# Two late modulation rows: from TensorE products to sums on VectorE

## The chip, the cores and the metric

One core of a Trainium2 chip runs the whole layer. The metric is the device time of one execution in microseconds (us), as the median of several runs; the profile is that of one further execution. The engines are called as the profile calls them: PE is TensorE's matmuls and PEld its weight loads, DVE is VectorE, ACT is ScalarE, POOL is GpSimd, and SP is the engine whose queue issues most of the DMA loads. Each engine works through its instructions in a fixed order and waits where an operand is missing.

## The reference, cut to what matters

The layer computes six modulation rows from one vector, uses two of them in the first norm, one as the gate of the first residual, two in the second norm and one as the gate of the second residual:

```python
mod = jax.nn.silu(c) @ w_ada[i] + b_ada[i]                  # (1, 1024) @ (1024, 6144)
sh1, sc1, g1, sh2, sc2, g2 = jnp.split(mod[:, None, :], N_MOD, axis=-1)
h = modulate(rmsnorm(x, norm1_g[i]), sh1, sc1)
...                                                          # projection, attention, long convolution
x = x + g1 * gated_merge(...)
h2 = modulate(rmsnorm(x, norm2_g[i]), sh2, sc2)
x = x + g2 * swiglu(h2, ffn_w1[i], ffn_w3[i], ffn_w2[i])
```

All is in float32. The parts are numbered 0 to 5 in the order of the split, so parts 2 and 5 are the gates g1 and g2, and parts 3 and 4 are the shift and scale of the second norm. The weight of one part is 1024 by 1024, 4 MB.

## The kernel before, in words

The kernel goes through these stages: the first norm and the input projection (40 chunks of 128 output columns; each chunk is two halves of 512 tokens, and a half is 24 products of 128x128 by 128x512, `gemm`, line 195); beside the projection a second stream of work, `side`; then attention, the merge of the branches, the second norm and the feed-forward network.

The second stream first makes the filters of the long convolution (`filters`) together with the late modulation rows (`ada_rows`, the function that is changed), and then runs the four convolutions (`conv`). `filters` goes four times through the same steps: products of the filter network (`filt_ps`, line 363) times a decay table that is loaded in tiles (`dec`, line 359; the product is `fv`, line 370), folds on DVE (lines 378 to 430, the last of them writes `a`), Fourier products on PE (`dft_ps`, lines 442 to 444), a copy by ACT, and a store of the spectrum by SP (`spec<-ks`, line 390). The convolutions use the same folds and Fourier products and begin with the load of `u` (line 454). Their tiles take the memory that the pool of the filters and the modulation rows has had.

The projection's weights come through one raw buffer (`wr`, loaded by SP, line 181), which ACT casts to a high part (`wh`, line 175) and DVE splits into a low part (`wl`, line 176). For the convolution's chunks DVE also adds the taps of a short convolution (line 600), and PE turns the result to tokens (`tm_ps`, line 569).

In `ada_rows` the rows are made in two pairs, (3, 4) and then (2, 5). For a pair, a row tile `arow` takes the biases from memory (line 882). For each part and each of the eight blocks k of 128 input channels, SP loads a weight tile `wal` of 128 by 1024 (512 KB, line 887), in three buffers. Four products (line 889) multiply it by the column of silu(c) of that block: the stationary operand is 128x32, with silu(c) in its first column, and each of the four works on 256 columns in a strip of 32 columns of the array, so part n of the pair ends up in rows 0, 32, 64 and 96 and columns 256n to 256n + 255 of one PSUM tile `ar_ps`, which is held until the pair is done. DVE adds it to `arow` (line 893), POOL writes the rows to memory (line 896). The first pair is then also turned into columns for the second norm. The gate rows are read back much later: g1 before the merge's output (line 1002), g2 in the feed-forward's second half (line 1367).

The order of the work is set in two steps. Generators yield estimated costs, and `_merged` takes the next step from the stream that is furthest behind its share; filters (97) and rows (39) are merged so, and the whole side stream (496) with the projection (39 chunks). The order that results is the order of the program. When the program is built, a planner with its own estimate of durations then gives each engine a fixed order: among what is ready and has its buffers it takes what comes first in the program, so that projections fill PE's time where a fold is not ready. Weight loads and taps are raised in priority; a few instructions are kept in program order.

Of the kernel before, what the change touches and what calls it, by code (L numbers as in the profile page):

```python
# [10 lines left out]
F32 = mybir.dt.float32  # L11
F32R = mybir.dt.float32r
AF = mybir.ActivationFunctionType
ALU = mybir.AluOpType
# [4 lines left out]
P = 128  # L19
D = 1024  # L20
# [138 lines left out]
class Block:  # L159
# [712 lines left out]
    def ada_rows(self, pool, psf):  # L872


        nc, a = self.nc, self.a
        for pair in ((3, 4), (2, 5)):
            r = pool.tile([P, 512], F32, tag="arow", name="arow", bufs=1)
            nc.gpsimd.memset(r, 0.0)
            for n, part in enumerate(pair):
                for j in range(4):  # L880
                    at = part * D + 256 * j
                    nc.gpsimd.dma_start(r[32 * j:32 * j + 1, 256 * n:256 * n + 256], a["b_ada"][0:1, at:at + 256])
            ps = psf.tile([P, 512], F32, tag="f", name="ar_ps")
            for n, part in enumerate(pair):
                for k in range(8):
                    w = pool.tile([P, D], F32, tag="wal", name="wal", bufs=3)
                    nc.sync.dma_start(w, a["w_ada"][k, :, part * D:(part + 1) * D])
                    for j in range(4):
                        nc.tensor.matmul(ps[32 * j:32 * j + 32, 256 * n:256 * n + 256], self.cs[:, 2 * k:2 * k + 32],
                                         w[:, 256 * j:256 * j + 256], start=(k == 0), stop=(k == 7),  # L890
                                         tile_position=(0, 32 * j))
                    yield 1.2
            nc.vector.tensor_add(r, ps, r)
            for n, part in enumerate(pair):
                for j in range(4):
                    nc.gpsimd.dma_start(self.modd[part][0:1, 256 * j:256 * j + 256],
                                        r[32 * j:32 * j + 1, 256 * n:256 * n + 256])
            if pair[0] == 3:
                pt = psf.tile([P, 512], F32, tag="f", name="ada_t")
                for j in range(4):  # L900
                    nc.tensor.transpose(pt[:, j * P:(j + 1) * P], r[:, j * P:(j + 1) * P], self.ident)
                v = pt.rearrange("p (n h g q) -> p n q g h", n=2, h=2, g=4)[:, :, 0]
                cols = lambda t: t.rearrange("p (g h) -> p g h", h=2)
                nc.vector.tensor_copy(cols(self.mod2[:, 1, :]), v[:, 0])
                nc.vector.scalar_tensor_tensor(cols(self.mod2[:, 0, :]), v[:, 1], 1.0, cols(self.ng[:, 1, :]),
                                               op0=ALU.add, op1=ALU.mult)
# [207 lines left out]
    def sums(self, wa, psf, xs, raw, h2):  # L1114

        nc = self.nc
        for k in range(4):
            b = []
            for kk in (k, k + 4):
                pt = psf.tile([P, 512], F32, tag="f", name="hT_ps")  # L1120
                for j in range(4):
                    mm = nc.tensor.transpose(pt[:, j * P:(j + 1) * P], xs[j][:, kk * P:(kk + 1) * P], self.ident)
                    if j == 0:
                        self.tc.keep_in_program_order(mm)
                h = wa.tile([P, 512], F32, tag="t", name="htmp")
                nc.scalar.activation(h, pt, AF.Identity, bias=self.mod2[:, 1, kk:kk + 1],
                                     scale=self.mod2[:, 0, kk:kk + 1])
                b.append(h)
            put = lambda n, src: self.split(h2[n][0][:, k, :], h2[n][1][:, k, :], src)
            b12, b22 = b  # L1130
            b11, b21 = raw[:, k, :], raw[:, k + 4, :]
            nc.vector.tensor_sub(b11, b12, b11)
            put(5, b11)
            nc.vector.tensor_sub(b12, b22, b12)
            put(7, b12)
            nc.vector.tensor_sub(b11, b22, b11)
            put(6, b11)
            put(3, b22)
            nc.vector.tensor_sub(b21, b21, b11)
            put(4, b21)  # L1140
            yield
# [312 lines left out]
```

## Time and profile before

| | before |
|---|---|
| median of 3 runs | 1719.76 us (1718.63 to 1722.28) |
| profiled execution | 1721.66 us, span 1719.9 us |
| PE busy | 1669.8 us, 97% of the span |
| DVE busy | 1187.3 us, 69% |
| ACT busy | 662.2 us, 39% |
| POOL busy | 152.7 us, 9% |
| mean granted TensorE clock | 0.995 |

The span goes from the first to the last instruction. Busy shares are means over stages that differ, so a stage has to be read by itself. The rows of a group give line, engine, operation, what is written and read, shape and count, then busy us and mean ns of one, then the idle time before them and what ended it. The filters and the modulation rows take the time from about 76 to 330 us of the span, the convolutions the time from there to about 660.

### The profile page before, as it was taken

How to read it: one execution, taken by the hardware profiler on the slowest of the kernel's cores; microseconds unless marked ns; L12 is line 12 of the kernel's file. 1: busy time of each engine (PE TensorE's matmuls, PEld its weight loads, DVE VectorE, ACT ScalarE, POOL GpSimd, SP SyncE). 2: the span in 40 equal slices, each digit the busy share in tenths (PEclk: the TensorE clock that was granted, in tenths of full speed). 3: DMA queues.
4: the chain of work that ended last, by engine and by line, in shares of the span. 5: the costliest groups of instructions: out<-in, count | busy, mean ns of one | idle time of the engine just before them, and what ended most of it. 6: DMA issues, size and time to landing. Idle time of an engine off the chain costs nothing.

```text
span 1719.9 us, 22909 instructions
## 1 busy us (share of the span) xinstructions
PE 1669.8 (97%) x8348; PEld 1311.0 (76%) x8348; DVE 1187.3 (69%) x2006; ACT 662.2 (39%) x1141; POOL 152.7 (9%) x273
## 2 busy tenths in 40 slices
PE   6999999999999999999999999999999999999997
PEld 2766766777777777888787788788888888878886
DVE  3665266699995966565865867867866566479566
ACT  4711222312221224455654325733333333355455
POOL 0100210101010004020200001010101001100000
PEclk9999999999999999999999999999999999999999
DMA  9375556645554456344657524333432323395344
GB/s 357 108 252 198 170 196 207 216 159 180 172 180 157 159 178 193 125 144 129 202 171 241 165 68 165 129 122 129 153 105 94 108 92 105 111 381 176 99 121 153
DMA packets 109910, 282.51 MB, mean 164 GB/s; under 512 B 15327, under 2 KB 24163, under 8 KB 107493
## 3 DMA queue, kind: packets, MB, share of 16 engines
q1 hardware_dynamic: 89864, 219.99, 38.2%
q0 software_dynamic: 19280, 60.60, 10.5%
q8 instruction: 66, 1.08, 0.3%
q10 hardware_dynamic: 653, 0.44, 0.1%
q14 instruction: 47, 0.39, 0.1%
HBM read 213.60 MB, written 67.39 MB: 163 GB/s over the span
## 4 chain that ended last, share of the span: by engine, by line
PE 44%; issue 26%; DVE 5%; DMA 5%; POOL 3%; ACT 1%; SPq 0%; POOLq 0%; ACTq 0%; DVEq 0%
PE in_ps L195 11%; PE out_ps L1091 5%; PE dx_ps L1322 5%; PE x_ps L1153 4%; PE dz_ps L1322 3%; PE dft_ps L442 2%; PE hy_ps L195 2%; PE pt_ps L800 2%; PE pt_ps L786 2%; PE na_ps L195 1%; POOL g L1266 1%; DMA ar<-g 1%; PE dft_ps L443 1%; PE dy_ps L1322 1%; PE dft_ps L444 1%
## 5 line engine op out<-in xcount | busy, mean ns | idle before, releaser
L195 PE MATMUL in_ps<-hTh,wl 128*128 128x512 f32 x640 | 259.3, 406 | 2.1 <-ACT proj L614 1.7
L195 PE MATMUL in_ps<-hTh,wh 128*128 128x512 f32 x640 | 253.2, 396 | 0.0
L195 PE MATMUL in_ps<-hTl,wh 128*128 128x512 f32 x640 | 252.6, 395 | 0.3 <-DVE hTl L176 0.2
L195 PEld LDWEIGHTS in_ps<-hTh,wl 128*128 128x128 f32 x640 | 120.7, 189 | 33.6 <-issue 5.1
L195 PEld LDWEIGHTS in_ps<-hTh,wh 128*128 128x128 f32 x640 | 120.8, 189 | 28.0 <-issue 1.6
L195 PEld LDWEIGHTS in_ps<-hTl,wh 128*128 128x128 f32 x640 | 120.9, 189 | 26.7 <-DVE hTl L176 1.9
L176 DVE TENSOR_TENSOR wl<-wr,wh 128x1024 fp32r<-128x1024 f32 (+1 forms) x56 | 59.8, 1068 | 95.7 <-ACT wh L175 95.6
L175 ACT CAST wh<-wr 128x1024 fp32r<-128x1024 f32 (+1 forms) x56 | 51.9, 926 | 135.6 <-PE in_ps L195 109.1
L176 DVE TENSOR_TENSOR ol<-ws,oh 128x512 fp32r<-128x512 f32 x88 | 60.4, 688 | 48.7 <-ACT oh L175 48.5
L176 DVE TENSOR_TENSOR ol<-ar,oh 128x512 fp32r<-128x512 f32 x77 | 52.8, 688 | 47.0 <-ACT oh L175 47.0
L175 ACT CAST oh<-ar 128x512 fp32r<-128x512 f32 x77 | 47.9, 622 | 83.6 <-PE dx_ps L1322 33.1
L175 ACT CAST oh<-ws 128x512 fp32r<-128x512 f32 x88 | 54.7, 622 | 57.5 <-PE x_ps L1153 27.4
L775 ACT ACTIVATE pe<-pe,mx 128x640 f32<-128x640 f32 x64 | 52.6, 823 | 49.3 <-DVE mx L774 49.3
L1322 PE MATMUL dx_ps<-ol,oh 128*128 128x512 f32 x176 | 68.7, 390 | 1.7 <-DVE ol L176 1.7
L442 PE MATMUL dft_ps<-a,matf 128*128 128x512 f32 x128 | 66.2, 598 | 4.0 <-DVE a L430 3.1
L1322 PE MATMUL dx_ps<-oh,ol 128*128 128x512 f32 x176 | 67.3, 390 | 2.0 <-DVE ol L176 2.0
L774 DVE CUSTOM_DVE_ANT_0 pe<-s_ps,bias 128x640 f32<-128x640 f32 x64 | 50.1, 820 | 27.7 <-PE s_ps L769 27.7
L1322 PE MATMUL dx_ps<-oh 128*128 128x512 f32 x176 | 68.5, 389 | 0.0
L175 ACT CAST oh<-wr 128x512 fp32r<-128x512 f32 x70 | 43.3, 622 | 51.5 <-PE x_ps L1153 16.0
L176 DVE TENSOR_TENSOR ol<-wr,oh 128x512 fp32r<-128x512 f32 x70 | 48.0, 688 | 21.2 <-ACT oh L175 21.0
L370 DVE TENSOR_TENSOR fv<-filt_ps,dec 128x512 f32<-128x512 f32 x32 | 21.5, 688 | 51.7 <-DMA dec<-in_decay 32.1
L1093 DVE TENSOR_TENSOR x<-x,out_ps 128x512 f32<-128x512 f32 x64 | 42.7, 684 | 19.1 <-PE out_ps L1091 18.9
(391 smaller groups left out, 4191.4 us busy)
## 6 DMA issues: line engine op xcount, KB each, us to landing
wr<-in_w SPq DMA_DIRECT2D x52, 512.0 KB, 3.6
wr<-in_w_in SPq DMA_DIRECT2D x40, 512.0 KB, 4.5
ar<-g SPq DMA_DIRECT2D x77, 256.0 KB, 2.8
wal<-in_w_ada SPq DMA_DIRECT2D x32, 512.0 KB, 6.6
matf<-in_dft_f SPq DMA_DIRECT2D x32, 384.0 KB, 4.4
bias<-in_rpb SPq DMA_DIRECT2D x64, 192.0 KB, 3.7
g<-t POOLq DMA_DIRECT2D x47, 256.0 KB, 3.0
w<-in_w SPq DMA_DIRECT2D x44, 256.0 KB, 5.4
```

The source lines that it names most:

```text
L175: self.nc.scalar.copy(hi, src)
L176: self.nc.vector.tensor_sub(lo, src, hi.bitcast(F32))
L195: mm = nc.tensor.matmul(ps, ww[:, k * P:(k + 1) * P], xx[:, k, pos:pos + width], start=(i == 0), stop=(i == n - 1))
L442: nc.tensor.matmul(ps, m[:, 0], v.rearrange("p a b -> p (a b)"), start=True, stop=False)
L774: nc.vector.tensor_tensor_reduce(pe, ps[:, 256:896], bt, -1.0, 3e38, ALU.add, ALU.min, mx[:, 0:1])
L775: nc.scalar.activation(pe, pe, AF.Exp, bias=mx[:, 0:1], scale=-1.0, accum_out=mx[:, 1:2])
L786: pin(nc.tensor.transpose(pt[:, at:at + P], pe[:, c * P:(c + 1) * P], self.ident))
L800: pin(nc.tensor.matmul(pt[ch, 1280:1408], vv[:, ch], pts[:, hh, c * P:(c + 1) * P], start=(c == 0), stop=(c == 4), tile_position=(0, 64 * ...
L1091: nc.tensor.matmul(ps, gg[x][:, tk], ww[y][:, sl], start=(i == 0), stop=(i == n - 1))
L1093: nc.vector.tensor_add(x1[:, sl], x1[:, sl], ps)
L1153: mm = nc.tensor.matmul(ps, w[u][:, k * P:(k + 1) * P], x[v][:, k, :], start=(start and k == 0 and i == 0), stop=(stop and k == 3 and i == 2),
L1322: nc.tensor.matmul(ps[j], x[u][:, j * P:(j + 1) * P], w[v], start=(start and i == 0 and c == 0), stop=(stop and i == N - 1 and k == len(re ...
```

## The change

The first pair, parts 3 and 4, is computed as before, now in the inner generator `products`. The second pair, the gates, goes through the new generator `sums`. It splits each part in two halves of 512 columns. For a half it loads eight tiles of 128 by 512 (256 KB) and sums them on DVE: the first is multiplied by its block's column of silu(c), and each further one is multiplied and added to the accumulator `aacc` (128x512). The accumulator still holds one sum for each of 128 partitions, so two products with a stationary block of ones (128x32) add over the partitions, 256 columns each, in two strips of 32; DVE adds the 64 rows that hold them to `arow`. The tag `wal` has two buffers for both pairs, where it had three; a half-width tile takes a full-width buffer. The yielded costs of the pair sum to the same 19.2. Biases, stores and everything behind stay.

```diff
 def ada_rows(self, pool, psf):
+        ones = pool.tile([P, 32], F32, name="ones", tag="ones", bufs=1)
+        nc.gpsimd.memset(ones, 1.0)
+        def products(r, pair):
+            ...
+                    w = pool.tile([P, D], F32, tag="wal", name="wal", bufs=2)
+            ...
+        def sums(r, pair):
+            for n, part in enumerate(pair):
+                for h in range(2):
+                    acc = pool.tile([P, 512], F32, tag="aacc", name="aacc", bufs=2)
+                    for k in range(8):
+                        w = pool.tile([P, D], F32, tag="wal", name="wal", bufs=2)[:, 0:512]
+                        at = part * D + 512 * h
+                        nc.sync.dma_start(w, a["w_ada"][k, :, at:at + 512])
+                        c = self.cs[:, 2 * k:2 * k + 1]
+                        if k:
+                            nc.vector.scalar_tensor_tensor(acc, w, c, acc, op0=ALU.mult, op1=ALU.add)
+                        else:
+                            nc.vector.tensor_scalar(acc, w, c, None, op0=ALU.mult)
+                        yield 0.6
+                    ps = psf.tile([P, 512], F32, tag="f", name="ar_ps")
+                    for j in range(2):
+                        g = 64 * h + 32 * j
+                        nc.tensor.matmul(ps[g:g + 32, 0:256], ones, acc[:, 256 * j:256 * j + 256], start=True,
+                                         stop=True, tile_position=(0, g))
+                    rs = r[64 * h:64 * h + 64, 256 * n:256 * n + 256]
+                    nc.vector.tensor_add(rs, ps[64 * h:64 * h + 64, 0:256], rs)
 ...
-            ps = psf.tile([P, 512], F32, tag="f", name="ar_ps")
-            for n, part in enumerate(pair):
-                for k in range(8):
-                    w = pool.tile([P, D], F32, tag="wal", name="wal", bufs=3)
-                    ...
-            nc.vector.tensor_add(r, ps, r)
+            yield from (products if pair[0] == 3 else sums)(r, pair)
```

More of the change, by code (lines that the diff above doesn't have):

```diff
@@ L875, in ada_rows @@
         nc, a = self.nc, self.a
+        ones = pool.tile([P, 32], F32, name="ones", tag="ones", bufs=1)
[5 more added lines that the diff above has]
+                    w = pool.tile([P, D], F32, tag="wal", name="wal", bufs=2)
+                    nc.sync.dma_start(w, a["w_ada"][k, :, part * D:(part + 1) * D])
+                    for j in range(4):
+                        nc.tensor.matmul(ps[32 * j:32 * j + 32, 256 * n:256 * n + 256], self.cs[:, 2 * k:2 * k + 32],
+                                         w[:, 256 * j:256 * j + 256], start=(k == 0), stop=(k == 7),
+                                         tile_position=(0, 32 * j))
+                    yield 1.2
+            nc.vector.tensor_add(r, ps, r)
+        def sums(r, pair):
+            for n, part in enumerate(pair):
+                for h in range(2):
+                    acc = pool.tile([P, 512], F32, tag="aacc", name="aacc", bufs=2)
+                    for k in range(8):
+                        w = pool.tile([P, D], F32, tag="wal", name="wal", bufs=2)[:, 0:512]
[7 more added lines that the diff above has]
+                        yield 0.6
+                    ps = psf.tile([P, 512], F32, tag="f", name="ar_ps")
+                    for j in range(2):
[4 more added lines that the diff above has]
+                    nc.vector.tensor_add(rs, ps[64 * h:64 * h + 64, 0:256], rs)
         for pair in ((3, 4), (2, 5)):
@@ L882, in ada_rows @@
                     nc.gpsimd.dma_start(r[32 * j:32 * j + 1, 256 * n:256 * n + 256], a["b_ada"][0:1, at:at + 256])
-            ps = psf.tile([P, 512], F32, tag="f", name="ar_ps")
-            for n, part in enumerate(pair):
-                for k in range(8):
-                    w = pool.tile([P, D], F32, tag="wal", name="wal", bufs=3)
[L887 to L893, printed above, removed]
+            yield from (products if pair[0] == 3 else sums)(r, pair)
             for n, part in enumerate(pair):
```

## The prediction

> **What bounds the kernel now.** I read the first part of the page, then the busy time of each engine by stretch (columns: stretch, its length, then busy us and instructions of PE, PEld, DVE, ACT, POOL; granted clock, DMA share, GB/s).
>
> ```profile
> span 1719.9 us, 22909 instructions
> PE 1669.8 (97%) x8348; PEld 1311.0 (76%) x8348; DVE 1187.3 (69%) x2006; ACT 662.2 (39%) x1141; POOL 152.7 (9%) x273
> ...
> 60.00:200.00 140.00, 131.18 (x713) 95.80 (x712) 74.73 (x107) 36.70 (x65) 14.92 (x28) 0.96 0.61 206
> 200.00:320.00 120.00, 116.59 (x634) 85.73 (x632) 69.66 (x99) 27.02 (x44) 18.01 (x30) 1.00 0.57 186
> 320.00:540.00 220.00, 220.00 (x925) 166.40 (x924) 193.14 (x336) 53.44 (x76) 17.86 (x25) 1.00 0.54 181
> ```
>
> TensorE has work nearly always: the gate pair runs in the second stretch, and there PE lacks 3.4 us of 120 while VectorE lacks 50.3. Only the convolutions behind it load both (VectorE 193 of 220). Next, what PE waited for over the whole span (total, times, longest), of which these are the waits around the change.
>
> ```profile
> PE dft_ps L442 <- DVE a L430: 3.1, 2, 2.7
> PE filt_ps L363 <- DVE fv L370: 2.9, 2, 2.4
> PE ar_ps L889 <- DMA wal<-in_w_ada: 2.7, 3, 1.7
> ```
>
> So I take PE for the bound: a microsecond of matmuls removed is one gained, unless a wait takes its place.
>
> **What goes from TensorE.** Sixteen steps of four products, each product two instructions. The products' groups, over both pairs and in the second stretch alone:
>
> ```profile
> L889 PE MATMUL ar_ps<-wal,cs 128*32 128x256 f32 x256 | 18.8, 387 | 2.8 <-DMA wal<-in_w_ada 2.7
> L889 PE MATMUL ar_ps<-wal,cs 128*32 128x256 f32 x120 | 9.0, 386 | 0.1
> ```
>
> Half of 18.8 is 9.4 us. PE's timeline (start, duration) checks this and gives the cost of a switch:
>
> ```profile
> 162.97 0.28 PE L195 MATMUL ctx_ps<-hcTh,wh 128*128 128x256 f32 x1
> 163.18 1.50 PE L889 MATMUL ar_ps<-wal,cs 128*32 128x256 f32 x24
> 164.61 0.50 PE L195 MATMUL in_ps<-hTh,wl 128*128 128x512 f32 x1
> ...
> 234.43 0.28 PE L195 MATMUL ctx_ps<-hcTh,wh 128*128 128x256 f32 x1
> 234.63 1.07 PE L889 MATMUL ar_ps<-wal,cs 128*32 128x256 f32 x16
> 235.64 0.50 PE L195 MATMUL in_ps<-hTh,wl 128*128 128x512 f32 x1
> ```
>
> From the matmul before to the one after is 1.64 us with three steps and 1.21 with two: 0.43 a step, and 0.35 for the rest, which holds the matmul before as well; I take 0.3 for a switch. Sixteen steps are 6.9 us without switches (lower bound); with the nine groups in which they come, 9.6. I take 9.4.
>
> **What comes to TensorE.** Four sums over partitions: a stationary block of ones, two products of 256 columns in two strips of the array, so four instructions where a step had eight in four strips. No row has this shape. The nearest with two strips is attention's value product, beside transposes of the same 128 columns that use the whole array:
>
> ```profile
> 743.19 1.31 PE L786 MATMUL pt_ps<-ident,pe 128*128 128x128 f32 x10
> 744.43 0.66 PE L800 MATMUL pt_ps<-pts,vc 128*64 128x128 f32 x8
> 744.92 0.82 PE L800 MATMUL pt_ps<-pts,v 128*64 128x128 f32 x12
> 745.67 0.50 PE L195 MATMUL in_ps<-hTh,wl 128*128 128x512 f32 x1
> ```
>
> Ten instructions took 1.24 us to the next start, and the twenty in strips of 64 took 1.24 too: two strips run side by side. So a sum costs what a step does, 0.43 and the 0.3 of the switch, 0.73; four are 2.9 us. Bounds: 1.7 (no switch) and 4.7 (the strips one after the other, 0.86 + 0.3).
>
> **What comes to VectorE.** By half part, one first product and seven multiply-adds on 128x512, and one add of 64x256; the old add of 128x512 goes. Durations from groups of these shapes:
>
> ```profile
> L504 DVE TENSOR_SCALAR e<-e 128x512 f32<-128x512 f32 x8 | 3.3, 418 | 0.1
> L507 DVE SCALAR_TENSOR_TENSOR wk<-e 128x512 f32<-128x512 f32 x8 | 5.5, 682 | 0.0
> L477 DVE TENSOR_TENSOR y<-t,t 128x256 f32<-128x256 f32 x32 | 13.3, 416 | 0.2
> L893 DVE TENSOR_TENSOR arow<-ar_ps,arow 128x512 f32<-128x512 f32 x2 | 1.4, 686 | 0.6 <-PE ar_ps L889 0.6
> ```
>
> 4 x (0.418 + 7 x 0.682 + 0.416) - 0.686 = 21.7 us more. The cover is the 50.3 us in which VectorE is idle from 200 to 320; without it the kernel would be 21.7 - 5.1 = 16.6 us slower. Behind each step stand, on VectorE's queue, the weight splits (wl, which PE's projections need) and the filter's folds (a, which PE's transforms need). From the old pair's place nothing has a near date: the gate rows are in memory at 318 and first read back at 915 (last fence). I take 0 for the path. Bounds: -3.4, since the bank that held the pair's products all that time is free now and PE's idle time there could go; +6.6 and a slower clock, below.
>
> **Loads.** Bytes stay; 16 loads of 512 KB become 32 of 256 KB on SP's queue, and both pairs have two buffers where there were three. Issues, KB and median us to landing:
>
> ```profile
> wal<-in_w_ada SPq DMA_DIRECT2D x32, 512.0 KB, 6.6
> dec<-in_decay SPq DMA_DIRECT2D x32, 256.0 KB, 3.9
> ```
>
> Two in flight at 3.9 us give a half step every 2 us, 62 us for 32, inside the stretch. SP has this in the stretch now:
>
> ```profile
> 286.87 12.93 SPq L887 DMA_DIRECT2D wal<-in_w_ada  x3
> 300.78 0.33 SPq L181 DMA_DIRECT2D wr<-in_w_in  x1
> ```
>
> Three loads that wait for their buffers hold SP for 13 us already, with the next weights (wr) behind them, and PE's waits shown above hold none for weights. Sixteen more issues of 0.33 us are 5.3 us of a queue that is mostly empty: 0.
>
> **The first pair**, still products, loses a buffer. Its groups of three (two of them, one shown at 163) must break: two more switches, 0.6. Each may meet a landing: between 0 and the longest such wait, 1.7, each; PE's three of them average 0.9, and half of the breaks meeting one gives 0.8. Together 1.4 (0 to 4.0).
>
> **Sum.** -9.4 + 2.9 + 0 + 1.4 = -5.1 us, against the profiled execution's own 1721.66 (span 1719.9 and 1.8 around it): 1716.6. That execution lies 1.9 above the median shown, so the median goes from 1719.76 to 1714.7.
>
> **A stall's real price.** What would undo this is a single PE wait of some size:
>
> ```profile
> 142.00:144.00 2.00, 0.25 (x1) 0.25 (x2) 0.69 (x1) 0.00 (x0) 0.00 (x0) 1.00 0.84 301
> 144.00:146.00 2.00, 1.50 (x7) 0.92 (x7) 0.69 (x1) 0.00 (x0) 0.00 (x0) 0.75 0.42 162
> 146.00:148.00 2.00, 2.00 (x7) 1.16 (x5) 0.69 (x1) 0.00 (x0) 0.00 (x0) 0.50 0.82 219
> 148.00:150.00 2.00, 2.00 (x6) 1.60 (x5) 0.69 (x1) 0.00 (x0) 0.00 (x0) 0.50 0.82 301
> 150.00:152.00 2.00, 2.00 (x6) 1.52 (x5) 0.69 (x1) 0.00 (x0) 0.00 (x0) 0.54 0.44 137
> 242.00:244.00 2.00, 1.99 (x7) 1.41 (x8) 2.00 (x4) 0.24 (x1) 0.71 (x1) 1.00 0.66 231
> ```
>
> The wait of 2.9 us on the filter's product (fv, itself late for its decay table) was followed by four windows at granted clocks of 0.75, 0.50, 0.50 and 0.54: 0.5 + 1.0 + 1.0 + 0.9 = 3.4 us more. One such wait costs 6.3. [...] This case's trace shows the drop behind 2.9 us, and none behind the wait of 2.7 (clock 1.00 from 242 on).
>
> **Rivals.** *VectorE starves on its loads (slower).* The filter's products are the model for an operation that is fed by two loads in flight:
>
> ```profile
> L370 DVE TENSOR_TENSOR fv<-filt_ps,dec 128x512 f32<-128x512 f32 x16 | 10.7, 687 | 28.1 <-DMA dec<-in_decay 17.6 <-PE filt_ps L363 10.5
> L176 DVE TENSOR_TENSOR wl<-wr,wh 128x1024 fp32r<-128x1024 f32 x5 | 6.1, 1224 | 18.7 <-ACT wh L175 18.7
> ```
>
> 17.6 us of landings for 16 operations, 1.1 each. The same for 32 multiply-adds is 35.2; with 21.7 of work 56.9, which is 6.6 more than VectorE has. It decides once work and waits together pass 50.3. The place is the handover, where the last spectra are stored and the convolution's first load waits for the filter's memory:
>
> ```profile
> 314.74 3.88 POOL L896 DMA_DIRECT2D mod<-arow  x8 [11.65 <-DVE arow L893]
> 322.58 5.92 SPq L390 DMA_DIRECT2D spec<-ks  x4
> 330.50 0.32 SPq L454 DMA_DIRECT2D u<-z  x1
> 915.60 0.53 POOL L1002 DMA_DIRECT2D g<-mod  x1 [3.47 <-DMA hyo<-ghy]
> ```
>
> Behind it VectorE is 88% full and can't catch up. If PE has no projection left to put in, 6.6 + 3.4 - 5.1 = +4.9: 1724.7. Against it: most of the idle time now is itself waiting (18.7 us of it for ACT's casts of weights, by the order of the queue), and a multiply-add put there costs nothing.
>
> *The gain is eaten (no change).* The first pair's waits at their bound, 4.0, and strips one after the other, 4.7: -9.4 + 4.7 + 4.0 = -0.7, 1719.1; or one stall with its clock drop, -5.1 + 6.3 = +1.2, 1721.0. For it: the convolutions' VectorE is nearly full, so time saved before 320 can be lost there. Here also belongs that the change doesn't shorten PE's path at all since another engine sets the convolutions' pace, 1719.8; against this, PE shows 220 of 220.
>
> *The episode at 143 goes.* With fewer loads ahead in the first pair, the decay tables may land sooner (DMA engines were 84% busy while PE waited): -5.1 - 6.3 = -11.4, 1708.4.
>
> **Chances.** The sum above 0.42; eaten 0.26; starving 0.22; the episode gone 0.10. About 0.2% (3.4 us) is what a measurement of this kernel tells from no change: faster 0.42 + 0.10 = 0.52, same 0.26, slower 0.22. The forecast's own range is 1712.1 (-9.4 + 1.7 and nothing for the first pair) to 1716.3, where faster ends; with the other cases 1708.0 to 1725.5.
>
> **What will show it.** Products of L889 at half their number, near 9.4 us, and four sums near 0.73 us each; 28 multiply-adds near 682 ns. VectorE's busy time from 200 to 320 up by about 20 us, and PE's waits for a, fv and wl not above some 3 us more in all. Right for the wrong reason if the windows at clock 0.5 behind 144 have gone. Wrong if PE waits for sums' loads through VectorE, if the first convolution's load comes later than 330, or if the projections run dry before the convolutions end.

## The result, and the profile after

The changed kernel takes 1729.72 us (median of 9 runs, 1721.89 to 1735.53) beside 1722.12 us before (9 runs, 1718.63 to 1728.82): a ratio of 1.0043, with a 95% interval of 1.0025 to 1.0060, so 7.4 us slower. The profiled execution has a span of 1727.9 us, 8.0 more than before.

The first part of the page, and busy time by stretch, with a stretch to 330 as well (columns as in the prediction; the first row of the second fence is the kernel before):

```profile
span 1727.9 us, 22772 instructions
PE 1669.1 (97%) x8236; PEld 1310.0 (76%) x8236; DVE 1210.3 (70%) x2041; ACT 662.6 (38%) x1141; POOL 152.8 (9%) x274
...
60.00:200.00 140.00, 129.69 (x699) 94.05 (x699) 75.32 (x108) 36.42 (x65) 14.98 (x29) 0.96 0.60 198
200.00:330.00 130.00, 119.73 (x548) 88.62 (x545) 93.54 (x135) 30.15 (x49) 18.09 (x29) 0.96 0.57 180
330.00:520.00 190.00, 189.30 (x802) 142.96 (x801) 171.90 (x300) 46.44 (x66) 17.04 (x24) 1.00 0.56 185
```

```profile
200.00:330.00 130.00, 126.59 (x673) 92.91 (x672) 73.60 (x105) 31.91 (x51) 19.59 (x32) 1.00 0.57 188
```

PE has 112 instructions less, and yet as much busy time: part of it ran at half clock (0.50 in windows shown below). In the stretch of the sums PE lacks 10.3 us of 130 where it lacked 3.4, and the clock of 0.96 takes up to 0.04 x 130 = 5.2 more (part of the slow time is idle time that is counted already). VectorE is 19.9 us busier there. Behind 330 little differs.

The groups of the change, by line (busy us, mean ns, then the idle time before and what ended it):

```profile
L888 PE MATMUL ar_ps<-wal,cs 128*32 128x256 f32 x128 | 9.6, 389 | 2.5 <-DMA wal<-in_w_ada 2.5
L911 PE MATMUL ar_ps<-aacc,ones 128*32 128x256 f32 x16 | 2.5, 391 | 0.0
L904 DVE SCALAR_TENSOR_TENSOR aacc<-wal,cs,aacc 128x512 f32<-128x512 f32 x28 | 21.0, 751 | 24.7 <-DMA wal<-in_w_ada 24.4
L906 DVE TENSOR_SCALAR aacc<-wal,cs 128x512 f32<-128x512 f32 x4 | 1.9, 480 | 4.6 <-DMA wal<-in_w_ada 4.6
L914 DVE TENSOR_TENSOR arow<-ar_ps,arow 64x256 f32<-64x256 f32 x4 | 1.7, 418 | 0.1
```

The work went and came as reckoned; new are 29.0 us in which VectorE stands still for the sums' loads. They aren't idle time on top: from 60 to 345 VectorE's waits for ACT's weight casts, the decay tables and the filter's products fall from 44.6 + 32.1 + 18.4 = 95.1 us to 24.2 + 25.2 + 4.5 = 53.9. So their sum alone says little; one has to see who stands behind a wait. Who then waits is in PE's list (the whole span):

```profile
PE filt_ps L363 <- DVE fv L370: 7.0, 4, 2.8
...
PE dft_ps L442 <- DVE a L430: 5.7, 4, 3.9
```

These were 2.9 and 3.1. One such stall as a chain, the load on SP's queue and VectorE's timeline first, then PE's:

```profile
269.08 0.64 SPq L901 DMA_DIRECT2D wal<-in_w_ada  x1
```

```profile
270.14 0.75 DVE L904 SCALAR_TENSOR_TENSOR aacc<-wal,cs,aacc 128x512 f32<-128x512 f32 x1
275.91 0.75 DVE L904 SCALAR_TENSOR_TENSOR aacc<-wal,cs,aacc 128x512 f32<-128x512 f32 x1 [5.02 <-DMA wal<-in_w_ada]
276.70 1.29 DVE L370 TENSOR_TENSOR fv<-filt_ps,dec 128x512 f32<-128x512 f32 x2
```

```profile
277.44 1.07 PE L363 MATMUL filt_ps<-fw,hid 64*128 64x256 f32 x4 [2.75 <-DVE fv L370]
```

```profile
276.00:278.00 2.00, 0.56 (x4) 0.48 (x5) 1.97 (x4) 0.00 (x0) 0.00 (x0) 0.91 0.56 217
278.00:280.00 2.00, 2.00 (x8) 1.15 (x5) 0.70 (x2) 0.00 (x0) 0.00 (x0) 0.50 0.81 222
280.00:282.00 2.00, 2.00 (x8) 1.61 (x7) 0.38 (x1) 0.00 (x0) 0.00 (x0) 0.74 0.57 161
```

The load starts when an earlier multiply-add has freed its buffer (it ends at 269.05), and lands 6.7 us after its issue, where the prediction counted 3.9 for a load of this size. A multiply-add waits 5.0 us for this tile; the filter's product `fv`, behind it on VectorE, frees PSUM late; PE waits 2.75 us, and then runs at 0.50 and 0.74 of its clock. The other stall is the old one of 2.7 us at 242, now 3.9 us, and the half clock that follows is new:

```profile
244.80 2.07 PE L442 MATMUL dft_ps<-a,matf 128*128 128x512 f32 x2 [3.91 <-DVE a L430]
```

```profile
244.00:246.00 2.00, 1.20 (x2) 0.68 (x3) 2.00 (x6) 0.00 (x0) 1.56 (x3) 0.50 0.81 262
246.00:248.00 2.00, 2.00 (x6) 1.20 (x5) 1.23 (x3) 0.00 (x0) 0.22 (x1) 0.50 0.23 67
248.00:250.00 2.00, 2.00 (x4) 0.95 (x3) 1.38 (x2) 0.58 (x1) 0.00 (x0) 0.50 0.00 0
```

At the handover the whole loss is there. The first convolution's load stood at 330.50; it is 8.4 us later, and the span 8.0:

```profile
329.26 6.68 SPq L390 DMA_DIRECT2D spec<-ks  x4
338.89 0.32 SPq L454 DMA_DIRECT2D u<-z  x1
```

### The profile page after: what moved, and what is told of

Read it like the earlier page. It is cut to its first block, busy times and chain, and to the rows that moved or that the text cites. A ratio compares the mean times of both kernels' runs of the same rounds, so it can differ in the third digit from the quotient of the medians.

```text
span 1727.9 us, 22772 instructions
## 1 busy us (share of the span) xinstructions
PE 1669.1 (97%) x8236; PEld 1310.0 (76%) x8236; DVE 1210.3 (70%) x2041; ACT 662.6 (38%) x1141; POOL 152.8 (9%) x274
## 3 DMA queue, kind: packets, MB, share of 16 engines
q0 software_dynamic: 19280, 60.60, 10.6%
## 4 chain that ended last, share of the span: by engine, by line
PE 45%; issue 28%; DMA 11%; DVE 10%; POOL 3%; ACT 2%; SPq 0%; POOLq 0%; DVEq 0%; ACTq 0%
PE in_ps L195 10%; PE out_ps L1121 5%; PE dx_ps L1352 5%; DMA wal<-in_w_ada 4%; PE x_ps L1183 4%; PE dz_ps L1352 3%; PE dft_ps L442 3%; PE hy_ps L195 2%; PE pt_ps L800 2%; PE pt_ps L786 2%; DMA dec<-in_decay 1%; PE dft_ps L443 1%; PE dft_ps L444 1%; POOL g L1296 1%; DMA wada<-in_w_ada 1%
## 5 line engine op out<-in xcount | busy, mean ns | idle before, releaser
L195 PEld LDWEIGHTS in_ps<-hTh,wh 128*128 128x128 f32 x640 | 120.7, 189 | 26.9 <-issue 0.7
L1123 DVE TENSOR_TENSOR x<-x,out_ps 128x512 f32<-128x512 f32 x64 | 42.6, 683 | 18.4 <-PE out_ps L1121 18.3
L1121 PE MATMUL out_ps<-wouh,ml 128*128 128x512 f32 x128 | 50.5, 394 | 1.8 <-DVE ml L176 1.3
```

The source lines that it names most:

```text
L195: mm = nc.tensor.matmul(ps, ww[:, k * P:(k + 1) * P], xx[:, k, pos:pos + width], start=(i == 0), stop=(i == n - 1))
L1121: nc.tensor.matmul(ps, gg[x][:, tk], ww[y][:, sl], start=(i == 0), stop=(i == n - 1))
L1123: nc.vector.tensor_add(x1[:, sl], x1[:, sl], ps)
```

## The experiments

All ratios are to the kernel before, run on the same chip; 0.1% is 1.7 us. The theories are named in the first expectation.

**Two buffers alone.**

```diff
-  w = pool.tile([P, D], F32, tag="wal", name="wal", bufs=3)
+  w = pool.tile([P, D], F32, tag="wal", name="wal", bufs=2)
```

> The kernel before, with two buffers for the weight tiles of both pairs instead of three, and nothing else: all parts stay products. Three theories of the 7.6 us that the change loses. S (starved): VectorE's multiply-adds wait for their loads (29 us in the changed kernel's trace), and what stands behind them on its queue comes late to TensorE. W (work): the 23 us more of work on VectorE, with no help from waits. F (first pair): the lost third buffer, by TensorE's own waits in the first pair. F expects this kernel slower than before by most of the loss, 4 to 8 us. S and W expect it within 2 us of before.

1.0019 (1.0003 to 1.0036): 3.3 us. PE's waits for the weight tiles rise from 2.7 us in 3 to

```profile
PE ar_ps L889 <- DMA wal<-in_w_ada: 6.2, 7, 1.8
```

So the lost buffer costs something, less than F expected, and is not the whole loss. It is no measure of the first pair alone: of these 6.2 us, 3.9 are waits from 193 us on, for the second pair's tiles, which the changed kernel doesn't multiply on PE. In the changed kernel PE's waits for the first pair's tiles are 2.5 us in 3, as before (2.7 in 3).

**One load for a half part.**

```diff
   for k in range(8):
-      w = pool.tile(...)[:, 0:512]; nc.sync.dma_start(w, ...)
+      if not k: w = pool.tile(...)[:, 0:512]; nc.sync.dma_start(w, ...)
```

> The changed kernel with one weight load for each half part instead of eight; all eight VectorE operations of the half read that one tile, so the gate rows are not the layer's. The work on VectorE stays, 28 of its 32 waits for a load go (and 28 of 32 loads). S expects the waits of the sums under 6 us and the time below before: by the sum of the prediction about 5 us below, 1717. W expects it to stay where the changed kernel is, 6 to 9 us above before.

0.9968 (0.9949 to 0.9986): 5.5 us faster than before, though VectorE does all the sums' work. The sums' waits are 3.3 us instead of 29.0, all of them before a first product, the one operation that still waits for a load, and the stretch shows neither much idle time of PE nor a clock drop:

```profile
200.00:330.00 130.00, 127.38 (x603) 96.83 (x602) 94.83 (x139) 34.09 (x54) 19.91 (x32) 1.00 0.47 154
```

W is out as the cause by itself: all the work fits in. What this run leaves open is whether the waits or the 28 loads, 7 MB of traffic, did the harm.

**Thin sums.**

```diff
-  nc.vector.scalar_tensor_tensor(acc, w, c, acc, ...)
+  nc.vector.scalar_tensor_tensor(acc[:, 0:32], w[:, 0:32], c, acc[:, 0:32], ...)
```

> The changed kernel with the 28 multiply-adds on 32 columns instead of 512 (the gate rows are mostly those of the first block of channels only); all loads, buffers and waits stay, and the order of the instructions is nearly the changed kernel's. A multiply-add should take about 0.1 to 0.25 us instead of 0.75, so some 15 us of work go. W expects the loss to go: 3 to 6 us below before. S expects VectorE to wait for the loads as before or longer (25 to 40 us) and the time to stay above before by 4 us or more.

1.0020 (1.0004 to 1.0037), 3.4 us slower, a little under what S gave. With 251 ns for a multiply-add, 14 us of work are gone, and VectorE's waits for the loads are longer:

```profile
DVE aacc L904 <- DMA wal<-in_w_ada: 28.4, 21, 4.3
...
DVE aacc L906 <- DMA wal<-in_w_ada: 10.6, 3, 4.7
```

PE's stretch is nearly as bad as in the changed kernel:

```profile
200.00:330.00 130.00, 121.41 (x555) 90.63 (x556) 81.91 (x138) 31.42 (x50) 18.88 (x30) 0.96 0.58 186
```

So the waits stop VectorE even when the sums give it little to do. The work may still have a part: 4 of the 7.4 us are back without it, though the two intervals (0.7 to 6.4 us here, 4.3 to 10.3 for the changed kernel) overlap.

**Four half tiles in flight.**

```diff
+  if k % 2 == 0:
+      w2 = pool.tile([P, D], F32, tag="wal", name="wal", bufs=2)
+      for i in range(2): nc.sync.dma_start(w2[:, 512 * i:512 * i + 512], a["w_ada"][k + i, :, at:at + 512])
+  w = w2[:, 512 * (k % 2):512 * (k % 2) + 512]
```

> The changed kernel with two half tiles in one weight buffer of 1024 columns, each still loaded by its own 256 KB load: four half tiles in flight in the memory in which there were two. Work, bytes and count of loads stay. S expects the sums' waits to fall from 29 us to 15 or less, and half of the loss or more to come back (within 3 us of before or below it). W expects no difference to the changed kernel, 6 to 9 us above before.

1.0020 (1.0006 to 1.0034): 3.4 us slower, about half of the loss back, just outside S's 3 us. The sums' waits are 14.3 + 4.7 = 19.0 us, less than before this edit but above the 15 expected. More in flight shortens the waits and doesn't cure.

**A third buffer in place of the accumulators.** Each multiply-add writes into its own weight tile and reads the previous one, so that no accumulator tile is needed. Three forms:

```diff
-  w = pool.tile([P, D], F32, tag="wal", name="wal", bufs=2)      # in both pairs
+  w = pool.tile([P, D], F32, tag="wal", name="wal", bufs=3)
   ...
-  acc = pool.tile([P, 512], F32, tag="aacc", name="aacc", bufs=2)
+  acc = None
   ...
-  nc.vector.scalar_tensor_tensor(acc, w, c, acc, op0=ALU.mult, op1=ALU.add)
+  nc.vector.scalar_tensor_tensor(w, w, c, acc, op0=ALU.mult, op1=ALU.add)
   ...
+  acc = w
```

Two half tiles a buffer, three buffers:

> The changed kernel without the accumulator tile: each multiply-add writes into its own weight tile and reads the tile before it, so that the memory of the accumulators makes a third weight buffer again, for both pairs; each buffer of 1024 columns holds two half tiles with a 256 KB load each, so up to five half tiles are in flight. S (VectorE starves on loads) with F (the first pair's lost buffer, 3 us by the run with two buffers alone) expects the sums' waits at 10 us or less, the first pair as before, and a time 3 to 6 us below before. If only the fixed order of the instructions is unlucky (O), the time stays 3 us or more above before whatever the waits are.

1.0007 (0.9987 to 1.0026): no difference to before. The waits are 15.8 + 3.9 = 19.7 us, not 10, and PE's stretch has 124.49 us busy at 0.97: the gain is there and is spent. S with F missed by 4 us and more; the 3 us or more above before that O expected didn't come either.

Undivided, 16 loads of 512 KB:

> As the chain of half tiles, but undivided: 16 loads of 512 KB in three buffers, 16 VectorE operations on 1024 columns, and two sums of four products each instead of four of two. Work on VectorE about 16 x 1.25 = 20 us, two switches of TensorE fewer. S and F expect the same as for the chain of half tiles, 3 to 7 us below before; if it is the halving that costs, this one is faster than that one by 2 us or more.

1.0043 (1.0028 to 1.0057), 7.4 us slower: a miss for S with F, and the halving is not what costs. VectorE still waits for the loads, in fewer and longer pieces, and PE has the longest wait of the three forms, with half clock behind it (0.50 from 244 to 246 us):

```profile
DVE wal L902 <- DMA wal<-in_w_ada: 18.6, 8, 5.2
```

```profile
PE dft_ps L442 <- DVE a L430: 5.9, 2, 5.5
```

Here the loss isn't at the handover: the first convolution's load is at 332.33, 1.8 us later than before, and the span is 7.8 longer. What PE has lost by then counts, not when that load goes out.

One half tile a buffer, three buffers, so two loads in flight:

> As the chain of half tiles, but one half tile to a buffer: three buffers, of which the accumulator's holds one, so two loads are in flight as in the changed kernel, while the first pair has its three buffers. S with F expects F's 3 us back and the rest of the loss to stay: 3 to 6 us above before, with the sums' waits at 20 us or more. If the first pair is the whole loss, this one is at or below before.

1.0007 (0.9996 to 1.0018), where S with F gave 3 to 6 us above before. The waits are 26.9 + 1.4 = 28.3 us, nearly the changed kernel's 29.0, and the time is 6 us better: PE's stretch is 122.69 us busy at 0.98. Compared with the changed kernel it has the first pair's third buffer, its loads for the sums begin at 169.7 us instead of 189.7, and its last multiply-add is at 323.0 instead of 294.6. PE's own waits for the first pair's tiles are not what is spared (3.0 us here, 2.5 there). Which of the rest spares PE isn't separated here. It shows that the sum of the waits doesn't set the loss by itself; that it is where they fall is likely, but not shown.

**The sums' loads on POOL's queue.**

```diff
-  nc.sync.dma_start(w, a["w_ada"][k, :, at:at + 512])
+  nc.gpsimd.dma_start(w, a["w_ada"][k, :, at:at + 512])
```

> The changed kernel with the 32 loads of the sums issued by POOL's queue instead of SP's; buffers and work stay. If what hurts is that the sums' loads stand ahead of the decay tables and weights on SP's queue (Q), the waits for decay tables fall by 10 us or more and half of the loss comes back. S expects the sums' waits to stay at 20 us or more and the time at 4 us or more above before.

1.0085 (1.0065 to 1.0106), 14.6 us slower. Q falls as far as this move can tell: VectorE's waits for decay tables hardly move (23.5 us, against 25.2), the sums' own are 36.8 (31.0 and 5.8), and PE has three half-clock spells after 240 (0.50 at 250 to 254, 282 to 286 and 314 to 316; 0.93 over the stretch). The move has a price of its own that isn't separated: POOL is busy 34.0 us in the stretch, where it was 18.1.

**All loads, none waited for.**

```diff
-  nc.vector.scalar_tensor_tensor(acc, w, c, acc, ...)
+  nc.vector.scalar_tensor_tensor(acc, acc, c, acc, ...)
```

> The changed kernel with all its 32 loads, in the same buffers and on the same queue, but the 28 multiply-adds read the accumulator itself instead of the weight tile (the gate rows hold only the first block of channels, scaled). Work on VectorE, bytes and buffers stay; only the waits of the 28 go. The run with one load a half took the traffic away as well, this one doesn't. If VectorE's waits are the cause (S), it is 3 to 7 us below before, like that run, with under 8 us of waits for the sums' loads. If it is the traffic of the loads (T: decay tables and weights land later), it stays 3 to 8 us above before.

0.9996 (0.9982 to 1.0010): 8 us faster than the changed kernel, at the time of before. Work, bytes, buffers and queue are the changed kernel's, and the 28 waits are gone. They are thus 8 of the 13 us between the changed kernel and the one with one load a half. Both S, which expected a time below before, and T, which expected one above, miss. So does S's figure for the waits that are left: 10.6 us in 2, not under 8. The other 5 us come with the 28 loads, so S alone doesn't hold. In this trace, which is of the slowest of the kernel's 12 runs (1726.33 us, median 1720.72), the filter's product waits more for its decay tables,

```profile
DVE fv L370 <- DMA dec<-in_decay: 34.7, 13, 7.3
```

against 23.7 in the kernel with one load a half (3.6 the longest), and the clock still drops once (0.50 from 242 to 248), at a wait of 6.5 us for a fold:

```profile
200.00:330.00 130.00, 122.08 (x570) 91.58 (x569) 92.87 (x135) 32.09 (x51) 19.89 (x32) 0.97 0.61 193
```

The kernel before loads the same bytes in this stretch and loses only 3.4 us of PE's time, so it isn't the bytes as such. On SP's queue the decay tables of one step go out in one row from 216.6 to 226.8 in the kernel with one load a half, and from 220.3 to 231.9 here, between the sums' loads. Whether this order, the traffic, or the other order of work that the planner makes for each form (the last multiply-add is at 274.1 here and at 294.6 in the changed kernel) costs the 5 us stays open.

**The sums on POOL.**

```diff
-  nc.vector.scalar_tensor_tensor(w, w, c, acc, op0=ALU.mult, op1=ALU.add)
+  nc.gpsimd.tensor_scalar(w, w, c, None, op0=ALU.mult); nc.gpsimd.tensor_tensor(w, w, acc, op=ALU.add)
```

> The chain of half tiles (three buffers, up to five half tiles in flight) with the sums on POOL instead of VectorE, as a multiply and an add each, 60 operations on 128x512; only the four adds from PSUM stay on VectorE. VectorE is then free of work and waits of the sums. If POOL takes about 1 us for an operation, 60 us of it lie beside the 107 us of the filters and the time is 4 to 7 us below before, the gain of the prediction's sum. Against it: POOL issues the stores of tokens and projections, which then wait behind the sums' loads; if the convolution's first load comes later by that, or if POOL takes 2 us and more for an operation, the time is above before.

1.0156 (1.0131 to 1.0180), 26.8 us slower. POOL's pair of operations takes 1.57 and 1.28 us in the median (up to 3.50 and 2.62), VectorE waits 28.1 us for a decay table once, and PE waits 18.4 us in one place:

```profile
PE ctx_ps L195 <- ACT tm L571: 18.4, 1, 18.4
```

No form that computes the layer is faster than the kernel before; the chain of half tiles and the chain with two loads in flight are level with it.

**All together.** What PE loses from 200 to 330 (not busy, plus 130 us times the missing share of the clock) goes with the time of the kernels. The removed products less the four sums, 18.8 - 9.6 - 2.5 = 6.7 us, are the gain against which it stands:

| kernel | PE's loss, us | more than before's 3.4, less 6.7 | span of this execution, against before's | measured, us |
|---|---|---|---|---|
| one load a half | 2.6 + 0 | -7.5 | -10.0 | -5.5 |
| loads not waited for | 7.9 + 3.9 | +1.7 | +4.6 | -0.7 |
| chain, half tiles | 5.5 + 3.9 | -0.7 | -4.3 | +1.2 |
| chain, two in flight | 7.3 + 2.6 | -0.2 | +3.7 | +1.2 |
| four in flight | 7.4 + 5.2 | +2.5 | +1.7 | +3.4 |
| thin sums | 8.6 + 5.2 | +3.7 | +5.8 | +3.4 |
| changed kernel | 10.3 + 5.2 | +5.4 | +8.0 | +7.4 |
| chain, undivided | 9.5 + 6.5 | +5.9 | +7.8 | +7.4 |
| loads on POOL's queue | 13.5 + 9.1 | +12.5 | +16.9 | +14.6 |
| sums on POOL | 31.9 + 15.6 | +37.4 | +25.3 | +26.8 |

The last column is a ratio of medians with an interval of some 3 us, the others are of one execution. Apart from the sums on POOL the account comes within 5 us of the time of both, which is enough for the large losses and not for the order of the small ones. Each form also has its own order of instructions from the planner; no run takes the waits away and keeps the order.

## Why the prediction was wrong, point by point

- *PE is the bound.* Right within the 5 us of the last table: the forms that lose more of PE's time in the stretch of the sums are the slower ones.
- *What goes and comes on TensorE.* Right: 9.6 us of products are left of two pairs' 18.8, and four sums cost 2.5 by their group (2.9 forecast). From the matmul before a sum to the one after are 0.77 us (235.25 to 236.02), as two strips side by side let expect. (The upper bound, 4 x (0.86 + 0.3), is 4.6 and not 4.7.)
- *What comes to VectorE.* Too small by a tenth: 751 ns for a multiply-add, where 682 was taken. The row used multiplies by a number in the instruction; the sums multiply by a column of a tile, and the row with that form was there to be read: the short convolution's taps on 128x512 took 745 ns. For the first product it is 480 instead of 418. Together 2.2 us, of no weight by itself.
- *"I take 0 for the path."* This step failed. Work of 24.6 us did fit into VectorE's idle time, as the kernel with one load a half shows. What didn't fit is the waiting in order, 29.0 us for loads: without 28 of the 32 waits the kernel is 8 us faster. That is 8 of the 12.5 us between the forecast of -5.1 and the measured +7.4. The case that was given 0.22, VectorE starving on its loads, is what happened. Its rate of 1.1 us a load forecast 35 us of waits; 29 came. Its price was +4.9, measured +7.4: the loss isn't one deficit at the handover, but two stalls, 241 to 245 and 275 to 277, with a clock drop to 0.50 behind each, where one drop was counted. And its reason, that work and waits exceed the idle time, isn't the right measure, since the kernel with two loads in flight and three buffers has nearly as long waits (28.3 us) and no loss that can be told from nothing.
- *Loads: 0.* As a change of queue or bytes it was right as far as tried: POOL's queue was worse, and undivided loads no better. But it took the loads' landing for harmless. The kernel in which nobody waits for 28 of them is level with before, not 5 us faster; only without those loads is it. These are the other 5 of the 12.5 us; the sum put them at nothing, and which property of the loads costs them stays open.
- *The first pair: 1.4 (0 to 4.0).* Too high, as far as the trace shows. Both groups of three broke, as forecast (at 107 and at 164), but no wait came with the breaks: PE's waits for the pair's tiles are 2.5 us in 3, where they were 2.7 in 3. That leaves two switches, 0.6 by the prediction's own estimate. (Half of two breaks at 0.9 would have been 0.9, not 0.8.) The 3.3 us of two buffers alone are for both pairs as products.
- *A stall's real price.* Right, and most of the loss: drops behind waits of 3.91 and 2.75 us take up to 5.2 us in the stretch. But the length of a wait alone doesn't decide whether the clock falls. The 2.9 us of the prediction were two waits, 2.41 and 0.51. A wait of 2.66 us left the clock alone before (1.00); with 2.75 us after, with 2.5 us in the chain of half tiles (at 221) and with 2.4 us with two buffers alone (at 142) it fell to 0.50. The 2.41 came behind products of the rows, the 2.75 behind products of the filter network, the 2.66 behind the projection's; whether that matters no run here separates, so what decides it is not shown.
- *The eaten gain; the episode at 143 gone.* Neither happened: the gain was more than eaten, and the clock over 60 to 200 is 0.96 in both kernels, the drop behind 144 with it.

## What to carry to other kernels

Idle time of an engine is no sure cover for work that waits for its own loads: the engine works in order, and a late operand holds up all that stands behind it, here the operations that feed TensorE (5.0 us of a multiply-add's wait, with `fv` behind it, became 2.75 us of PE's). Count, for work moved to a busy engine's gaps, its waits first and its work second, and read a row for them from an operation that is fed in the same way; here it was on the page (17.6 us for 16). Where TensorE is the bound, a wait can cost twice its length: before the change 2.9 us of waits cost some 6.3 by the prediction's sum, with the clock granted at 0.75, 0.50, 0.50 and 0.54 behind them, while one of 2.66 us had no drop behind it.

## What the runs showed of the hardware that had not been expected

A multiply-add with a scalar from a tile takes 751 ns on 128x512 where one with a constant takes 682. POOL takes 1.57 us for a multiply and 1.28 us for an add of 128x512 in float32 (medians; the profile's times for POOL are rough), where VectorE's add takes some 0.69 us. With waits of 2.4, 2.5 and 2.75 us the clock fell to 0.50, with one of 2.66 us it stayed at 1.00. A load of 256 KB landed after 3.5 us in the median of the changed kernel, and after 6.7 us ahead of the stall at 275.
